# A two-layer trunk on one core: two PSUM banks each for transposes and attention outputs, earlier raw weight loads, and sums of squares issued in smaller pieces

## The chip, the cores and the metric

The kernel runs on one core of one Trainium2 chip. The number compared is the device time of one execution in microseconds. The kernel before took 2080.81 us, the median of three runs from 2080.38 to 2085.92 us. Beside these there is one profiled execution, from which every row below comes.

A core has a matrix engine (TensorE: PE in the rows, PEld for its weight loads), VectorE (DVE), ScalarE (ACT), GpSimd (POOL) and SyncE (SP), which here only issues transfers. TensorE writes only to PSUM, which holds eight banks of 128 x 512 floats. VectorE and ScalarE empty the banks. Each engine runs its own instructions in the order in which the program has them, and waits on semaphores for the others.

## The reference

The input is one sequence of 1024 tokens with 1024 features, and 256 memory tokens. Two layers follow each other. In each, the stream is RMS-normed and put through one input projection. One half of the heads is a token mixer (a gated linear recurrence in layer 0, forgetting attention in layer 1), the other half is a cross-attention into the memory. Both outputs are concatenated, put through an output projection and added to the stream. Then a squared-ReLU MLP of width 4096 is added. In short:

```
for layer in range(2):
    h = rms_norm(x, norm_mix[layer])
    y_mix, xq = rglru_group(h, ...) if layer == 0 else fox_group(h, ...)
    y_mem = memory_group(xq, mem, ...)
    x = x + concat([y_mix, y_mem]) @ w_out[layer]
    x = x + square(relu(rms_norm(x, norm_mlp[layer]) @ w1)) @ w2

# fox_group, one block of queries
s = q @ k.T * scale + c[q] - c[k];  s = where(causal, s, -1e30)
o = softmax(s) @ v
```

All of it is in float32. The forgetting attention has 8 heads of 64 features, and the cross-attention 4 heads of 128.

## The kernel before

**Numbers.** Every operand of a product is kept as a rounded high part and a low part, and a product is three matmuls (high x high, high x low, low x high). A tile to be split is copied by ScalarE into the high part, and VectorE subtracts it to get the low part (`split_sb`, `split`, and for weights `_wpart`, lines 320 and 321).

**Stages.** The sequence is worked in two halves of 512 tokens (h = 0 and 1). In order of time: layer 0's projections, recurrence and cross-attention for both halves; its output projection (`outproj`, then `outproj2` for the second half); the MLP of layer 0 (`mlp`, about 345 to 927 us); layer 1's projections (`fox_proj`, `xq_proj`), its cross-attention (`xattn`) and forgetting attention (`fox`); its output projection; the MLP of layer 1 (from about 1465 us). The MLP treats its matrices as 2 x 2 blocks and computes them with seven block products instead of eight (`product`, line 1066), in eight groups g = 0 to 7, each with `mlp_z` (first matrix) and `mlp_out` (second).

**The forgetting attention.** For each head `fox_scores` computes four rows of scores (L1477, mask L1479) into an `s` bank. VectorE adds the decay and takes the minimum in one custom instruction (L1482), ScalarE takes the exponential with its sum (L252), VectorE the reciprocal (L1492), and GpSimd scales the row (L1494). `fox_pv` then turns these rows: for each block of 128 keys it transposes up to four 128 x 128 pieces into a `pt` bank (L1519), ScalarE copies the bank to the high part (L1522), VectorE subtracts for the low part (L1523), and two matmuls (L1509 with the high part, L1510 with the low) add the block into the head's `o` bank. At the end of a head ScalarE and VectorE empty the `o` bank (L1535, L1536). `fox_pair` (L1436, L1447) turns queries and keys of two heads through `pt` banks. In the first half a head has 4 key blocks, in the second 8.

**What sets the order.** The program is written as generators that are woven into each other: a stage of projections or output products runs as the main stream, and attention is advanced beside it at rates from the table `TUNE`. From the written program a scheduler then makes each engine's final order, moving an instruction where its operands and a free buffer are expected. A PSUM tile takes its bank from its tag's own small pool, `PB = {"pj": 2, "s": 2, "pt": 3, "o": 1}`: a third `pt` tile can be open while two are being emptied, but the next head's first L1509 must wait until the one `o` bank is empty. Matmuls of projections and of the MLP that are placed between attention's instructions are called filler below: they need nothing from the attention.

**Weights.** Raw chunks of 128 x 1024 floats go by SyncE's queue into three or four raw buffers (`_wraw`, L316), are split into one of three high and low buffers, and are then used. `_wraw(self.wload + 2)` issues loads for chunks less than two ahead of the last one split, and never into a buffer whose chunk isn't split yet. Layer 1's weights that both halves use are written to memory once split and read back.

**Sums of squares.** For the norm ahead of an MLP, `sq_pe` squares the eight tiles of the second half and `sq_mm` adds each by four matmuls with one output column (L467) into an `o` tile. Before, `sq_mm` is called inside the MLP's first group (in `hook0`) and around the waiting products in `mlp`.

**The last group of layer 0's MLP.** `held` keeps the first half of the stream in on-chip tiles `xres`: `plus` on VectorE (L1082) adds the first use of each bank into the tile, and later the second use. Elsewhere the first use is a ScalarE copy (`copies`, L1077), and the second is added to the copy.

Of the kernel before, what the change touches and what calls it, by code (L numbers as in the profile page):

```python
# [126 lines left out]
def chain(*gs):  # L127
# [33 lines left out]
    "cp_f00": 0,  # L161
    "cp_f01": 1,
    "cp_f10": 1,
    "cp_f11": 1,
    "cp_kv0": 1,
# [10 lines left out]
class Builder:  # L176
    NU = 86
    NRING = 3
    PB = {"pj": 2, "s": 2, "pt": 3, "o": 1}

    def __init__(self, ctx, tc, ins, out):
# [45 lines left out]
        warm = self.psum("pt")  # L227
        for _ in range(8):
            nc.tensor.matmul(warm[:, :P], lhsT=self.ones, rhs=self.ones, start=True, stop=True)
# [93 lines left out]
    def _wsplit(self, upto):  # L323
        nc = self.nc
        while self.wload < min(len(self.plan), upto):
# [19 lines left out]
            self.wload += 1  # L345
            self._wraw(self.wload + 2)

# [103 lines left out]
    def sq_pe(self, m, h, xt, behind=None):  # L451
        sq = self.F.get()
        i = self.nc.scalar.activation(sq[:, :H], xt, AF.Square)
        if behind is not None:
            self.after(i, behind)
        if m == 0:
            self.stp[h] = [None, []]
        self.stp[h][1].append((m, sq))

    def sq_mm(self, h, keep):  # L460
# [501 lines left out]
    def outproj2(self, h, k0, k1, src, gain, side):  # L962
        nc = self.nc
        tags = ["pj", "pj", "s", "s", "pt", "pt", "pt"]
        n = len(tags)
# [236 lines left out]
    def mlp_out(self, l, g, mid, side=None):  # L1202
# [28 lines left out]
        def held(a):  # L1231
            def first(q, ps):
                self.plus(self.xres[2 * q + a], ps)

            def then(q, ps):
                x = self.xres[2 * q + a]
                self.plus(x, ps)
                nc.sync.dma_start(self.xs[2 * q + a, :, :H], x[:, n])

# [31 lines left out]
        A = [self.psum(k) for k in ("s", "s", "pj", "pj")]  # L1271
        more = ("pt", "pt", "pt", "o")
        c11, c21, c22 = keep(0, 0), keep(1, 0), keep(1, 1)
# [11 lines left out]
    def mlp(self, l, wait, nxt=None):  # L1285
# [3 lines left out]
        def hook0(key):  # L1289
            if key in ahead:  # L1290
                self.xsplit(ahead[key])
            if key in ("b11", "b21"):
                self.sq_mm(1, 6 if key == "b11" else 3)
            if key in ("t2", "t3"):
                advance(nf)

        def hook7(key):
# [4 lines left out]
            if key == "t1" and l:  # L1302
                self.acc = [self.load_x(2 * q, 0, self.xs) for q in range(4)]

        for p in wait:
            for k in ("t3", "t1"):
                self.xsplit(k)
            self.sq_mm(1, 5)
            drain(p)
            self.sq_mm(1, 2)  # L1310
        for g in range(8):
            if g == 0 and g in self.parked:
                for k in ("t3", "t1"):
                    self.xsplit(k)
            drain(self.mlp_z(l, g, hook0 if g == 0 else hook7 if g == 7 else lambda key: None))
            if g == 7:
# [549 lines left out]
```

## Time and profile before

| | |
|---|---|
| median of three runs | 2080.81 us |
| the profiled execution | 2081.96 us |
| its span, first to last instruction | 2080.3 us |
| TensorE busy | 2046.6 us, 98% of the span |
| VectorE, ScalarE, GpSimd busy | 75%, 55%, 22% |
| mean granted TensorE clock | 0.996 |

A row of grouped instructions reads: line, engine, operation, output<-inputs (buffer numbers left out), shape, count | busy time, mean ns of one | idle time of the engine just before them and what ended it. A row of waits reads: who <- whom, us in total, times, longest. A row of the timeline reads: start, duration, engine, line, what, count, and in brackets the idle time just before and what ended it. A row of windows reads: stretch and length, then busy time with count for PE, PEld, DVE, ACT and POOL, the granted clock, the DMA engines' busy share and GB/s. Matmuls are pipelined, so their durations overlap: the distance from start to start counts, not the duration of one.

### The profile page before, as it was taken

How to read it: one execution, taken by the hardware profiler on the slowest of the kernel's cores; microseconds unless marked ns; L12 is line 12 of the kernel's file. 1: busy time of each engine (PE TensorE's matmuls, PEld its weight loads, DVE VectorE, ACT ScalarE, POOL GpSimd, SP SyncE). 2: the span in 40 equal slices, each digit the busy share in tenths (PEclk: the TensorE clock that was granted, in tenths of full speed). 3: DMA queues.
4: the chain of work that ended last, by engine and by line, in shares of the span. 5: the costliest groups of instructions: out<-in, count | busy, mean ns of one | idle time of the engine just before them, and what ended most of it. 6: DMA issues, size and time to landing. Idle time of an engine off the chain costs nothing. (4 is left out here: it accounts for less than half of the span.)

```text
span 2080.3 us, 29644 instructions
## 1 busy us (share of the span) xinstructions
PE 2046.6 (98%) x10378; PEld 1706.1 (82%) x10378; DVE 1569.0 (75%) x2924; ACT 1148.5 (55%) x2164; POOL 456.6 (22%) x582
## 2 busy tenths in 40 slices
PE   9999999999999999999999999999999999999999
PEld 7998778888788878879998998777778888888887
DVE  7897698776766776778685779686886767758757
ACT  7856655554553554547555646575655545545543
POOL 1022220202202201204442423232021222022021
PEclk9999999999999999999999999999999999999999
DMA  8433261635635635737767437644356575265274
GB/s 294 150 95 119 100 208 61 132 81 112 132 81 111 132 81 112 160 103 224 274 240 272 138 118 283 228 134 150 101 119 143 129 167 115 71 139 113 70 182 121
DMA packets 122645, 301.55 MB, mean 145 GB/s; under 512 B 13760, under 2 KB 15872, under 8 KB 122496
## 3 DMA queue, kind: packets, MB, share of 16 engines
q1 hardware_dynamic: 80736, 211.50, 30.1%
q0 software_dynamic: 41760, 88.16, 22.3%
q8 instruction: 81, 1.33, 0.3%
q14 instruction: 68, 0.56, 0.1%
HBM read 190.46 MB, written 109.15 MB: 144 GB/s over the span
## 5 line engine op out<-in xcount | busy, mean ns | idle before, releaser
L1066 PE MATMUL pspt<-r,wh 128*128 128x512 f32 x1536 | 493.4, 397 | 6.4 <-DVE f L1082 2.9
L321 DVE TENSOR_TENSOR wl<-wr,wh 128x1024 fp32r<-128x1024 f32 (+2 forms) x354 | 338.3, 964 | 182.7 <-ACT wh L320 181.5
L320 ACT ACTIVATE wh<-wr 128x1024 fp32r<-128x1024 f32 (+3 forms) x403 | 303.5, 776 | 301.6 <-PE pss L1066 77.0
L1222 POOL DMA_DIRECT2D xspill<-f x232 | 203.1, 1071 | 871.6 <-DVE f L1082 802.5
L1066 PEld LDWEIGHTS pspt<-r,wh 128*128 128x128 f32 x1536 | 288.2, 188 | 78.6 <-ACT r L500 4.3
L1066 PE MATMUL pss<-r,wh 128*128 128x512 f32 x1024 | 328.4, 397 | 0.5 <-DVE r L503 0.4
L1066 PE MATMUL pspt<-r,wl 128*128 128x512 f32 x768 | 304.0, 396 | 0.7 <-DVE wl L321 0.7
L1066 PE MATMUL pspj<-r,wh 128*128 128x512 f32 x832 | 273.6, 402 | 0.9 <-DVE r L495 0.7
L389 PE MATMUL pspj<-wh,r 128*128 128x256 f32 (+1 forms) x1280 | 244.3, 285 | 2.1 <-DVE fl L1390 0.8
L503 DVE TENSOR_TENSOR r<-f,r 128x512 fp32r<-128x512 f32 x282 | 188.6, 685 | 71.8 <-DMA xspill<-f 52.0
L1066 PEld LDWEIGHTS pss<-r,wh 128*128 128x128 f32 x1024 | 192.5, 188 | 48.3 <-DVE r L503 1.3
L500 ACT ACTIVATE r<-f 128x512 fp32r<-128x512 f32 x282 | 169.2, 625 | 79.0 <-DMA xspill<-f 20.4
L389 PEld LDWEIGHTS pspj<-wh,r 128*128 128x128 f32 x1280 | 201.8, 189 | 4.7 <-PE pspj L389 1.0
L1066 PE MATMUL pss<-r,wl 128*128 128x512 f32 x512 | 202.7, 396 | 0.0
L1066 PEld LDWEIGHTS pspj<-r,wh 128*128 128x128 f32 x832 | 157.0, 190 | 40.3 <-DVE r L495 1.6
L389 PE MATMUL pspj<-wl,r 128*128 128x256 f32 (+1 forms) x640 | 182.2, 285 | 0.6 <-DVE wl L321 0.3
L1066 PEld LDWEIGHTS pspt<-r,wl 128*128 128x128 f32 x768 | 144.5, 188 | 36.1 <-DVE wl L321 1.1
L1066 PE MATMUL pspj<-r,wl 128*128 128x512 f32 x416 | 165.4, 398 | 0.0
L389 PE MATMUL pspj<-r,wh 128*128 128x512 f32 x480 | 158.6, 406 | 1.8 <-ACT wh L320 0.9
L1087 ACT ACTIVATE f<-f 128x512 f32<-128x512 f32 x128 | 78.7, 626 | 109.2 <-DVE f L1086 107.0
L389 PEld LDWEIGHTS pspj<-wl,r 128*128 128x128 f32 x640 | 120.8, 189 | 1.6 <-DVE wl L321 0.5
L1066 PEld LDWEIGHTS pss<-r,wl 128*128 128x128 f32 x512 | 96.3, 188 | 23.4
(301 smaller groups left out, 3555.9 us busy)
## 6 DMA issues: line engine op xcount, KB each, us to landing
wr<-in_w_dram SPq DMA_DIRECT2D x136, 512.0 KB, 4.0
xspill<-f POOLq DMA_DIRECT2D x232, 256.0 KB, 7.4
f<-xspill SPq DMA_DIRECT2D x88, 256.0 KB, 4.7
xspill<-f SPq DMA_DIRECT2D x56, 256.0 KB, 3.2
wsp<-wh SPq DMA_DIRECT2D x22, 512.0 KB, 5.7
wsp<-wl SPq DMA_DIRECT2D x22, 512.0 KB, 6.1
wh<-wsp POOLq DMA_DIRECT2D x21, 512.0 KB, 5.7
wl<-wsp POOLq DMA_DIRECT2D x21, 512.0 KB, 5.6
```

The lines of the kernel that those rows point to most:

```text
L320: self.wact = self.nc.scalar.activation(hi, raw, AF.Copy)
L321: eng.tensor_tensor(lo, raw, hi.bitcast(F32), ALU.subtract)
L389: self.lastmm = self.nc.tensor.matmul(out, lhsT=a, rhs=b, start=(j == 0), stop=(j == n - 1))
L500: i = self.nc.scalar.activation(hi[:, :n], src, AF.Copy)
L503: self.nc.vector.tensor_tensor(lo[:, :n], src, hi[:, :n].bitcast(F32), ALU.subtract)
L1066: self.lastmm = self.nc.tensor.matmul(ps, lhsT=a, rhs=b, start=(start and c == 0 and j == 0), stop=(c == n - 1 and j == 2), skip_group_che ...
L1087: self.lastsq = self.nc.scalar.activation(f[:, n], f[:, n], AF.Square)
L1222: nc.gpsimd.dma_start(self.xs[2 * q + a, :, b * H:(b + 1) * H], f[:, n], accum_op=ALU.add)
```

## The change

It has six parts. (1) `PB` becomes two `pt` banks and two `o` banks; the places that named three `pt` tiles and one `o` (`outproj2`, `mlp_out`) now name two and two, or use an `o` for the last one. (2) Raw loads may be issued for chunks less than four ahead. (3) `sq_pe` calls `sq_mm` itself and keeps at most four squares back; `feed` issues one square at each step of the waiting products and of the MLP's groups, and the calls in `hook0` and `mlp` go. (4) In `held` the first use of a bank is a ScalarE copy; after the second use VectorE adds the bank, and then the copy, into `xres`. (5) Three of layer 1's four projections copy their raw PSUM tiles by ScalarE (L601) and no longer by VectorE (L599). (6) Ten warm-up matmuls stand at the start and not eight.

```
-    "cp_f01": 1,
-    "cp_f10": 1,
-    "cp_f11": 1,
+    "cp_f01": 0,
+    "cp_f10": 0,
+    "cp_f11": 0,
...
-    PB = {"pj": 2, "s": 2, "pt": 3, "o": 1}
+    PB = {"pj": 2, "s": 2, "pt": 2, "o": 2}
...
-        for _ in range(8):
+        for _ in range(10):
             nc.tensor.matmul(warm[:, :P], lhsT=self.ones, rhs=self.ones, start=True, stop=True)
...
             self.wload += 1
-            self._wraw(self.wload + 2)
+            self._wraw(self.wload + 4)
...
         self.stp[h][1].append((m, sq))
+        self.sq_mm(h, 4)
...
-        tags = ["pj", "pj", "s", "s", "pt", "pt", "pt"]
+        tags = ["pj", "pj", "s", "s", "pt", "pt", "o"]
...
         def held(a):
-            def first(q, ps):
-                self.plus(self.xres[2 * q + a], ps)
+            dst = []
+            first = self.copies(dst)
 
             def then(q, ps):
                 x = self.xres[2 * q + a]
                 self.plus(x, ps)
+                self.plus(x, dst[q][:, n])
+                self.F.put(dst[q])
                 nc.sync.dma_start(self.xs[2 * q + a, :, :H], x[:, n])
...
-        more = ("pt", "pt", "pt", "o")
+        more = ("pt", "pt", "o", "o")
...
-            if key in ("b11", "b21"):
-                self.sq_mm(1, 6 if key == "b11" else 3)
...
+        def feed(p):
+            for _ in p:
+                if 1 in self.stp:
+                    self.sq_mm(1, max(0, len(self.stp[1][1]) - 1))
...
-            self.sq_mm(1, 5)
-            drain(p)
-            self.sq_mm(1, 2)
+            feed(p)
...
-            drain(self.mlp_z(l, g, hook0 if g == 0 else hook7 if g == 7 else lambda key: None))
+            feed(self.mlp_z(l, g, hook0 if g == 0 else hook7 if g == 7 else lambda key: None))
```

Counted over the built programs, instructions change by kind only in (4), (5) and (6): VectorE loses 24 copies of 128 x 256, and ScalarE gets 24 of them and 8 copies of 128 x 512; eight of VectorE's additions read an on-chip tile where they read a bank. The matmuls are the same but for the two warm-ups. What moves is the order. From line 459 on, lines of the changed kernel are numbered one higher than before (L1509 is L1513 from line 1233 on). In the rows below, `pt`, `pj`, `s` and `o` after `ps` are the tags, and the number is that of the tile.

TensorE where the seventh head of the first half gives way to the eighth (time 1201 to 1204 us in the profile before). Before, the last filler and the eighth head's first products, with the `o` tile 11717:

```order
L389 MATMUL pspj_12041<-wl_77,r_1033_10211 128x264
L389 MATMUL pspj_12041<-wh_74,r_1034_10212 128x264
L1509 MATMUL pso_11717<-r_1190_11723,r_1035_10278 128x512
L1510 MATMUL pso_11717<-r_1191_11724,r_1035_10278 128x512
L1509 MATMUL pso_11717<-r_1193_11747,r_1036_10306 128x384
L1519 MATMUL pspt_11795<-ident,f_1185_11654 128x128
```

With the change, the same place, with the `o` tile 11735:

```order
L389 MATMUL pspj_12633<-wh_74,r_1011_9981 128x256
L1513 MATMUL pso_11735<-r_1198_11741,r_1043_10297 128x512
L389 MATMUL pspj_12633<-wl_77,r_1011_9981 128x256
L389 MATMUL pspj_12633<-wh_74,r_1012_9982 128x256
L389 MATMUL pspj_12633<-wh_74,r_1016_10019 128x256
L389 MATMUL pspj_12633<-wl_77,r_1016_10019 128x256
L389 MATMUL pspj_12633<-wh_74,r_1017_10020 128x256
L389 MATMUL pspj_12633<-wh_74,r_1021_10057 128x256
L389 MATMUL pspj_12633<-wl_77,r_1021_10057 128x256
L389 MATMUL pspj_12633<-wh_74,r_1022_10058 128x256
L1514 MATMUL pso_11735<-r_1199_11742,r_1043_10297 128x512
```

The product with the high part and that with the low part now have filler between them, and the `o` tile is in the bank that the head before does not use.

VectorE in the last group of layer 0's MLP (time 914 to 928 us before). Before, from the first additions of the banks `s` and `pj` on; `L1082` in each row is `plus`:

```order
L1082 TENSOR_TENSOR f_830_7865<-f_830_7865,pss_8006 128x512
L1187 TENSOR_TENSOR f_816_7732<-f_842_7970,f_816_7732 128x512
L1082 TENSOR_TENSOR f_832_7869<-f_832_7869,pspj_8008 128x512
L503 TENSOR_TENSOR r_841_7953<-f_823_7822,r_840_7952 128x512
L1082 TENSOR_TENSOR f_831_7867<-f_831_7867,pss_8007 128x512
L1187 TENSOR_TENSOR f_817_7746<-f_846_7992,f_817_7746 128x512
L1082 TENSOR_TENSOR f_833_7871<-f_833_7871,pspj_8009 128x512
```

With the change, the stretch that ends with the first addition from a `pt` bank, which before came nine rows behind the piece above:

```order
L504 TENSOR_TENSOR r_863_8115<-f_816_7734,r_862_8114 128x512
L504 TENSOR_TENSOR r_865_8119<-f_817_7748,r_864_8118 128x512
L504 TENSOR_TENSOR r_845_7979<-f_843_7976,r_844_7978 128x512
L1083 TENSOR_TENSOR f_830_7867<-f_830_7867,pspt_8057 128x512
L504 TENSOR_TENSOR r_857_8062<-f_842_7972,r_856_8061 128x512
L1083 TENSOR_TENSOR f_831_7869<-f_831_7869,pspt_8058 128x512
L1083 TENSOR_TENSOR f_832_7871<-f_832_7871,pso_8059 128x512
L1199 TENSOR_TENSOR f_823_7825<-f_823_7825,f_847_7998 128x512
L1083 TENSOR_TENSOR f_833_7873<-f_833_7873,pso_8060 128x512
```

From the low part of a weight that both programs split just ahead (`wl_77`) to this first addition, 16 instructions stand before and 14 with the change: the four additions from `s` and `pj` are gone, and one split (L504) and one subtraction (L1199) have come ahead of it.

TensorE in the second half of the forgetting attention. Before, ahead of the sixth head (about 1404 us), where transposes of one head go to three tiles in turn, with filler around them:

```order
L1066 MATMUL pspj_14842<-r_1504_14384,wh_75 128x512
L1519 MATMUL pspt_14246<-ident,f_1467_14137 128x128
L1519 MATMUL pspt_14255<-ident,f_1467_14137 128x128
L1519 MATMUL pspt_14295<-ident,f_1467_14137 128x128
L1066 MATMUL pspj_14842<-r_1505_14385,wh_75 128x512
L1066 MATMUL pspj_14842<-r_1504_14384,wl_78 128x512
```

With the change, where one of the heads without filler gives way to the next:

```order
L1523 MATMUL pspt_13688<-ident,f_1387_13514 128x128
L1523 MATMUL pspt_13688<-ident,f_1395_13579 128x128
L1513 MATMUL pso_13399<-r_1399_13608,r_1242_12290 128x128
L1514 MATMUL pso_13399<-r_1400_13609,r_1242_12290 128x128
L1523 MATMUL pspt_13697<-ident,f_1367_13381 128x128
L1523 MATMUL pspt_13697<-ident,f_1374_13434 128x128
L1523 MATMUL pspt_13697<-ident,f_1387_13514 128x128
L1523 MATMUL pspt_13697<-ident,f_1395_13579 128x128
L1481 MATMUL pss_13719<-r_1110_10905,r_1380_13479 128x512
L1481 MATMUL pss_13719<-r_1110_10905,r_1381_13480 128x512
L1513 MATMUL pso_13687<-r_1410_13693,r_970_9578 128x512
```

The transposes fill one tile, then the other, and no third; the next head's output has its own bank. Of the eight heads of the second half, counted from a head's first product to the next head's, three (the second, the third and the sixth) now have none of the filler matmuls (L389, L1066 before) between them; before, the head with the fewest has 12 (the sixth). The attention of the end of the first half stands up to 180 rows later against the projections, and has caught up again by the fourth head of the second half.

## The prediction

> **What bounds the kernel now.** I read the busy shares first, then a stretch of MLP in the chain of waits, then the waits of TensorE summed by releaser (who <- whom), and last the windows and timelines around those waits.
>
> ```profile
> PE 2046.6 (98%) x10378; PEld 1706.1 (82%) x10378; DVE 1569.0 (75%) x2924; ACT 1148.5 (55%) x2164; POOL 456.6 (22%) x582
> 1560.46 5.60 PE pspt L1066 x24
> PE pss L1477 <- DVE mn L1482: 4.7, 9, 1.3
> PE pspt L1066 <- DVE f L1082: 2.9, 2, 2.3
> PE pso L1509 <- DVE f L1536: 1.7, 1, 1.7
> ```
>
> TensorE bounds it. A matmul with 512 columns goes by every 5.60 / 24 = 0.233 us, and over the whole span TensorE idles 2080.3 − 2046.6 = 33.7 us. Since the change removes no matmul, it can win only there or where the clock is lower. The named idle places are few: in sum 4.7 us behind the attention's decay addition (L1482), 2.9 behind `plus` at the end of layer 0's MLP, 1.7 behind the emptying of the one `o` bank. Behind two of them the clock falls:
>
> ```profile
> 924.90:928.40 3.50, 1.90 (x5) 0.95 (x6) 3.50 (x7) 0.89 (x2) 0.00 (x0) 1.00 0.44 165
> 928.40:931.90 3.50, 3.50 (x10) 2.72 (x9) 3.50 (x7) 0.23 (x1) 0.00 (x0) 0.51 0.57 162
> 1201.50:1204.90 3.40, 1.65 (x10) 1.08 (x8) 3.40 (x6) 0.92 (x3) 0.39 (x1) 1.00 0.02 5
> 1204.90:1208.40 3.50, 3.50 (x19) 3.50 (x18) 2.22 (x8) 1.47 (x3) 0.00 (x0) 0.51 0.00 0
> 1471.20:1474.60 3.40, 3.40 (x9) 2.65 (x9) 3.40 (x7) 1.26 (x2) 0.00 (x0) 0.50 0.20 77
> 1484.80:1491.70 6.90, 6.12 (x14) 4.08 (x15) 6.25 (x11) 3.82 (x7) 0.00 (x0) 0.51 0.29 106
> ```
>
> After a stretch with 1.6 to 1.9 us idle, the next 3.4 us have a granted clock of 0.51. At that clock 3.4 us hold the work of 1.7, so such a period costs at most 1.7 us; I take 1.5, for the part in which TensorE would wait anyway. There are five such periods (the last row holds two).
>
> **The change part by part.** The sum is made against the profiled execution, 2081.96 us, which is 1.15 above the median of the three runs.
>
> *`held` (4).*
>
> ```profile
> 925.65 0.47 PE L1066 MATMUL pspt<-r,wh 128*128 128x512 f32 x1 [2.26 <-DVE f L1082]
> 924.84 0.67 DVE L1082 TENSOR_TENSOR f<-f,pspt 128x512 f32<-128x512 f32 x1
> 926.04 1.27 DVE L1082 TENSOR_TENSOR f<-f,pspt 128x512 f32<-128x512 f32 x2
> ```
>
> TensorE waits 2.26 us until VectorE reaches the first addition from a `pt` bank. VectorE is the late one: it has no gap here, and starts one of these instructions every 0.60 us (924.84 and 926.04, with one between). By the order shown above, 16 of its instructions stand ahead of that addition and 14 with the change: −1.2 us. The bounds are 0 (the two that are newly ahead wait for ScalarE) and −2.9, both waits. ScalarE has to fit in four copies; it is busy 55% of the span and 0.89 of the 3.50 us from 924.9, so it should have room, and if it hasn't, the wait goes over to it. With the gap under about half of its size, the window at 924.9 has 2.4 us busy and I expect no half clock: −1.5, between 0 and −1.5. The eight extra additions on VectorE come after the banks are free; no matmul waits for `xres` then.
>
> *Second `o` bank (1).*
>
> ```profile
> 1203.78 0.47 PE L1509 MATMUL pso<-r,r 128*128 128x512 f32 x1 [1.71 <-DVE f L1536]
> 1200.30 2.74 DVE L1372 TENSOR_TENSOR f<-f,fr 128x512 f32<-128x512 f32 x3
> 1202.97 0.67 DVE L1536 TENSOR_TENSOR f<-f,pso 64x512 f32<-64x512 f32 x1
> ```
>
> Here the emptying of the bank (L1536) stood behind three additions that take 2.74 us, and the next head's first product waited 1.71 us. With two banks it need not wait, and by the order filler stands between the products too: −1.7 (0 if the wait goes over to the `pt` banks), and the half-clock period from 1204.9 goes with it: −1.5 (0 to −1.5).
>
> *Raw loads (2).*
>
> ```profile
> 276.16 3.45 SPq L542 DMA_DIRECT2D f<-xspill  x3
> 279.71 0.37 SPq L316 DMA_DIRECT2D wr<-in_wout_dram  x1
> 283.68 0.63 ACT L320 ACTIVATE wh<-wr 128x512 fp32r<-128x512 f32 x1 [2.21 <-DMA wr<-in_wout_dram]
> 284.36 0.74 PE L978 MATMUL pspt<-r,wh 128*128 128x512 f32 x2 [0.57 <-ACT wh L320]
> ```
>
> A weight chunk of layer 0's output projection was issued behind three loads of the stream, its split waited 2.21 us for it, and TensorE 0.57. With the change this load stands ahead of those: −0.6, 0 to −0.6. The price: the load of a buffer waits on SP's queue until that buffer is split, and the stream's loads queue behind it. In the MLP a stream load has whole block products to land, so I take 0; if each of the two layers has one late as here, it is +1.1.
>
> *Two `pt` banks in the attention (1).* The first half has filler nearly everywhere. The second half doesn't:
>
> ```profile
> 1257.00:1453.00 196.00, 187.27 (x1002) 152.63 (x1002) 151.58 (x376) 122.62 (x273) 59.92 (x89) 1.00 0.59 201
> 1405.00:1423.00 18.00, 15.37 (x87) 12.29 (x87) 14.60 (x47) 11.94 (x32) 6.98 (x12) 1.00 0.30 102
> L389 PE MATMUL pspj<-r,wh 128*128 128x512 f32 x139 | 46.0, 404 | 0.2 <-ACT r L500 0.2
> L1066 PE MATMUL pspj<-r,wh 128*128 128x512 f32 x112 | 38.6, 409 | 0.7 <-DVE r L495 0.7
> L389 PE MATMUL pspj<-r,wl 128*128 128x512 f32 x69 | 27.6, 400 | 0.0
> L1066 PE MATMUL pspj<-r,wl 128*128 128x512 f32 x56 | 22.1, 394 | 0.0
> L389 PE MATMUL pspj<-wh,r 128*128 128x256 f32 x53 | 10.2, 284 | 0.0
> L1523 DVE TENSOR_TENSOR r<-pspt,r 128x512 fp32r<-128x512 f32 (+1 forms) x64 | 36.0, 583 | 9.4 <-ACT r L1522 9.2
> L1482 DVE CUSTOM_DVE_ANT_0 f<-pss,f 128x512 f32<-128x512 f32 x32 | 21.9, 684 | 0.6 <-DMA f<-cscr 0.5
> L1482 DVE CUSTOM_DVE_ANT_0 f<-pss,f,mn 128x128 f32<-128x128 f32 (+3 forms) x32 | 17.4, 544 | 4.8 <-DMA f<-cscr 3.2 <-PE pss L1479 1.2
> L1490 DVE TENSOR_TENSOR fsm<-fsm 128x1 f32<-128x1 f32 x32 | 6.3, 197 | 2.8 <-ACT f L252 2.6
> L1452 DVE SCALAR_TENSOR_TENSOR r<-pspt,gk,r 64x512 fp32r<-64x512 f32 x8 | 6.0, 750 | 0.3
> L1536 DVE TENSOR_TENSOR f<-f,pso 64x512 f32<-64x512 f32 x8 | 5.5, 683 | 5.4 <-ACT f L1535 5.3
> L1442 DVE SCALAR_TENSOR_TENSOR r<-pspt,par,r 64x512 fp32r<-64x512 f32 x7 | 5.2, 750 | 1.4 <-ACT r L1441 1.2
> L1482 DVE DVE_READ_ACCUMULATOR2_ANT mn<- 128x1 f32 x64 | 5.2, 82 | 0.0
> L1492 DVE RECIPROCAL frc<-fsm 128x1 f32<-128x1 f32 x32 | 5.1, 160 | 1.7
> ```
>
> These 196 us hold the eight heads; TensorE idles 8.7 us in them. Filler is 376 matmuls at 0.233 and, with half as many for the low part as the 53 shown, 79 of 256 columns at half of that: 87.6 + 9.2 = 96.8 us, which leaves (187.3 − 96.8) / 8 = 11.3 us of TensorE per head. VectorE's own rows for the attention (the last nine) sum to 108.6, or 13.6 per head. So a head without filler is set by VectorE, and TensorE idles 2.3 us in it even where VectorE never stops. VectorE does stop for ScalarE's copy ahead of L1523: 9.4 us, 1.2 a head; with a `pt` bank less to run ahead in, I take 0.8 of this into the head: 3.1 idle. Three heads have lost all their filler: 9.3 us. The 8.7 of now came mostly from the same limit in heads with little filler; with the filler now in the other five I let it go altogether: +0.6. From below, all idle but the three heads' 2.3 goes and the clock is better: 6.9 − 8.7 = −1.8. From above, a head lasts as long as the worst stretch of now, 18 us from 1405: see the third rival.
>
> *Parts at nothing.*
>
> ```profile
> 1150.00:1200.00 50.00, 50.00 (x403) 48.93 (x403) 42.27 (x143) 33.02 (x88) 21.58 (x35) 1.00 0.49 160
> 1.12 3.78 PE L229 MATMUL pspt<-ones 128*128 128x128 f32 x16 [1.12 <-DVE halo L815]
> 5.79 1.22 PE L389 MATMUL pspj<-r,wh 128*128 128x512 f32 x2 [0.89 <-ACT wh L320]
> ```
>
> (5) moves 24 copies of some 0.4 us off VectorE: in the first half's attention VectorE is busy 42 of 50 us and ScalarE 33, and TensorE waits for neither (50.00 busy). If ScalarE's ten more microseconds fell ahead of an exponential, they would show as VectorE's wait on it. (6) adds two matmuls (16 records for eight, 0.47 each): 0.94 in a gap of 0.89 in which TensorE waits for the first weight. (3) leaves its blocks at the start of layer 1's MLP almost as they are in the order, 12, 4, 8 and 8 products of L467 in one piece; if they were spread, the three half-clock periods from 1471 would go, −4.5. In the MLP four banks are emptied in about four times 0.6 us, while the next product runs 5.6, so two `pt` and two `o` do what three and one did.
>
> Sum: −1.2 − 1.5 − 1.7 − 1.5 − 0.6 + 0.6 = −5.9. 2081.96 − 5.9 − 1.15 = **2074.9 us** for the median.
>
> On the clock, the Trainium skill (page "TensorE: Matmul & The Clock Gate", Part 1: The HAM clock gate) says that the half rate comes after at least one idle window of about 3.4 us, and warns of gaps over that. This trace differs: stretches of 3.4 us that are half busy are followed by 0.51. By the page's rule gaps of this size would not move the clock, the two terms of 1.5 would be 0, and the time that of the second rival.
>
> **The rivals.** *The attention gains too.* Two `o` banks let the next head's scores and products start under the emptying of the last, and the idle 8.7 halves (−4.4 and not +0.6), and two of the three late half-clock periods go (−3.0): −13.9, **2066.9**. For it: L1536 waits 5.4 us on ScalarE's copy in these heads. Against: VectorE's 13.6 per head stays, and three heads have no filler.
>
> *The gaps go, the clock stays.* The half-clock periods move to other gaps: the sum is −1.2 − 1.7 − 0.6 + 0.6 = −2.9, **2077.9**. For it: there are periods after 1471 and 1484 that I cannot tie to one wait. Against: two of the five follow a gap that I can name.
>
> *Two transposing banks starve the heads without filler.* L1519 of the next block waits until L1523 has emptied the bank two back; with the third bank gone this is met at each block of the three heads (2, 3 and 6 of the second half). If each lasts 18 us, as 1405 to 1423 does, TensorE idles 18 − 11.3 = 6.7 in each, and being under two thirds busy it falls to half clock once per head (1.5): 3 × 8.2 − 8.7 = +15.9 in place of +0.6, sum +9.4, **2090.2**. It makes the kernel slower from heads of 16.9 us on. For it: TensorE idled 2.6 of 18 us there with three banks and some filler. Against: the chain of one block (0.6 for the copy, 0.6 for the subtraction) is shorter than a block's share of VectorE, 13.6 / 8 = 1.7, so two banks should feed it.
>
> **How the numbers follow.** Forecast 0.48, attention gains 0.17, clock stays 0.13, starved heads 0.22. A measurement of this kernel can tell about 0.3%, 6.2 us, from no change: faster is below 2074.6, slower above 2087.0. The forecast, at 2074.9, lies on that line: 0.24 faster, 0.24 the same. With the first rival 0.41 faster, with the second 0.37 the same, with the third 0.22 slower. The likeliest case's own range is 2070 to 2080, from its bounds; the range for 8 in 10 reaches to the first rival and almost to the third: 2065 to 2088.
>
> **What would show it.** Right: no wait at the first `pt` product near 924 above 1.1 us and clock 1.00 after it; no wait L1509 <- L1536; heads 2, 3 and 6 of the second half at about 14.4 us with waits of L1477 on L1482, not of L1519 on L1523; TensorE idle about 9 us in the second half. Wrong: waits L1519 <- L1523 (1523 and 1527 then) over 5 us, half-clock periods inside the second half's heads, waits of stream or `cscr` loads on SP behind raw loads, or ScalarE's copies at 916 to 924 late.

## The result, and the profile after

| | before | changed |
|---|---|---|
| median | 2083.36 us (4 runs, 2080.38 to 2086.63) | 2110.18 us (4 runs, 2107.93 to 2112.93) |
| ratio | | 1.013, 95% interval 1.0117 to 1.0142 |
| profiled execution | 2081.96 us | 2107.93 us |
| mean granted clock | 0.996 | 0.991 |

The change makes the kernel 27 us slower. The forecast was 2074.9 us, with a range up to 2088; it named the direction wrongly. The page of the changed kernel begins with its busy row, and the rows below it are from TensorE's waits over the whole span:

```profile
PE 2057.3 (98%) x10382; PEld 1710.6 (81%) x10382; DVE 1563.3 (74%) x2900; ACT 1164.2 (55%) x2196; POOL 449.9 (21%) x582
PE pss L1481 <- DVE mn L1486: 9.1, 9, 2.0
PE pspj L389 <- DVE wl L321: 4.4, 5, 2.0
PE pspt L389 <- DVE wl L321: 2.5, 1, 2.5
PE pspt L1523 <- DVE r L1446: 2.5, 2, 1.9
PE pso L1513 <- ACT r L1526: 1.8, 1, 1.8
```

(L1481, L1486, L1513 and L1523 are the L1477, L1482, L1509 and L1519 of before.) The wait for the emptied `o` bank (L1509 on L1536, 1.7 us) is gone, and of the 2.9 us behind `plus` 0.5 are left. TensorE's idle time has nevertheless grown from 33.7 to 2106.2 − 2057.3 = 48.9 us, and its busy time by 11 us, although it has only two more matmuls. That second part is the clock: at half clock a matmul is busy for longer.

Where the time went is seen by setting the same matmul of both traces against each other, the n-th of its line in order of time (the matmuls of L1066 are those of the MLPs):

| TensorE reaches | before, us | changed, us | late by |
|---|---|---|---|
| in layer 0's first output projection (L389, 1051st) | 238.1 | 239.3 | 1.3 |
| first product of `outproj2`, layer 0 (L978) | 259.9 | 275.2 | 15.3 |
| layer 0's MLP, 201st matmul of L1066 | 369.2 | 380.5 | 11.3 |
| end of that MLP's middle (2401st) | 883.1 | 893.9 | 10.8 |
| after its last group (2601st) | 935.4 | 941.3 | 5.9 |
| layer 1's first score (L1477) | 1116.4 | 1124.3 | 7.9 |
| first product of the second half's heads (L1509, 33rd) | 1286.0 | 1325.5 | 39.5 |
| layer 1's MLP (L1066, 3201st) | 1567.8 | 1593.9 | 26.1 |
| last matmul | 2075.3 | 2101.4 | 26.2 |

So there are two losses, of about 10 us at layer 0's output projection and of about 18 us in layer 1's attention up to the start of its MLP, and one gain of 5 us at the end of layer 0's MLP; 1.3 us come before these and 2 in layer 1's projections. (The 39.5 us at the first head of the second half is not all lost: filler that before stood behind that point has been done ahead of it.) The windows of the changed kernel show how: first the output projection of layer 0, then heads 1 to 6 of the second half, each from its first product to the next head's, and last all eight heads together (columns as in the windows of the prediction):

```profile
250.00:300.00 50.00, 43.78 (x181) 33.56 (x180) 40.53 (x67) 23.20 (x37) 5.52 (x6) 0.97 0.52 169
1325.50:1348.50 23.00, 19.59 (x97) 15.30 (x96) 15.16 (x31) 16.10 (x29) 4.52 (x8) 0.93 0.48 151
1348.50:1364.60 16.10, 13.83 (x73) 10.84 (x71) 12.08 (x42) 10.29 (x30) 5.85 (x10) 0.89 0.11 33
1364.60:1384.40 19.80, 14.39 (x64) 9.97 (x63) 13.16 (x35) 13.75 (x30) 3.76 (x6) 0.81 0.08 28
1384.40:1410.60 26.20, 26.20 (x134) 21.89 (x133) 20.24 (x62) 17.10 (x41) 10.06 (x16) 0.95 0.44 109
1410.60:1433.40 22.80, 21.40 (x115) 16.95 (x113) 19.21 (x51) 16.32 (x36) 5.10 (x9) 1.00 0.49 154
1433.40:1445.40 12.00, 10.02 (x59) 7.57 (x58) 9.08 (x29) 8.60 (x24) 4.30 (x7) 1.00 0.14 44
1325.00:1480.00 155.00, 140.31 (x707) 110.75 (x705) 106.76 (x282) 98.31 (x219) 40.76 (x67) 0.94 0.35 106
```

The heads without filler (2, 3 and 6: second, third and sixth row of the heads) last 16.1, 19.8 and 12.0 us, and TensorE idles 2.3, 5.4 and 2.0 us in them. VectorE isn't full in them either: 13.16 of 19.8 us in head 3. Over the heads the idle time is 155.0 − 140.3 = 14.7 us. Before, the same stretch, from 1286 to 1451 us, had 7.7:

```profile
1286.00:1451.00 165.00, 157.30 (x823) 126.98 (x822) 122.89 (x305) 103.20 (x228) 48.50 (x76) 1.00 0.54 183
```

The clock column is the other half: 1.00 before, 0.94 now. 0.06 of 155 us is 9 us of work not done, at most, since TensorE also idles in these periods. In heads 2, 3 and 6 VectorE waits for the decay rows, 3.3, 2.3 and 1.7 us of the 4.0, 6.6 and 2.9 that it idles there; in head 3 more of its waiting is for ScalarE's copies (3.2 us, L1527 on L1526). This is its timeline in heads 2 and 3 of the changed kernel, with the row of the queue that brings the rows:

```profile
1356.23 23.88 SPq L1466 DMA_DIRECT2D f<-cscr  x3
1359.17 0.69 DVE L1486 CUSTOM_DVE_ANT_0 f<-pss,f 128x512 f32<-128x512 f32 x1 [1.73 <-DMA f<-cscr]
1360.60 0.35 DVE L1486 CUSTOM_DVE_ANT_0 f<-pss,f,mn 128x128 f32<-128x128 f32 x1 [0.73 <-DMA f<-cscr]
1382.74 0.69 DVE L1486 CUSTOM_DVE_ANT_0 f<-pss,f 128x512 f32<-128x512 f32 x1 [1.79 <-DMA f<-cscr]
```

At the start of a head's scores VectorE stands still for the load, the scores' bank isn't emptied, and TensorE waits behind it (1.95 and 1.70 us at 1359.9 and 1383.5). The waits of VectorE and of SP over the second half sum to the first four rows; the last row is that of before:

```profile
DVE r L1527 <- ACT r L1526: 13.2, 14, 2.3
DVE f L1486 <- DMA f<-cscr: 10.0, 9, 1.8
SPq L1466 <- PE pspt L1523: 32.6, 4, 15.0
SPq L1466 <- PE pso L1514: 25.8, 2, 22.4
DVE f L1482 <- DMA f<-cscr: 3.7, 3, 3.2
```

The load itself waits on SP, by the rows mostly for transposes and products of earlier heads (L1523, L1514), before a buffer is free for it.

In layer 0 the trace suggests a chain of engines that each work in order. In time order, in the changed kernel:

```profile
251.47 2.56 ACT L252 ACTIVATE f<-f,sp 128x512 f32<-128x512 f32 x4 [2.17 <-PE pso L760]
252.28 1.23 POOL L893 TENSOR_SCALAR f<-f 128x512 f32<-128x512 f32 x2 [3.97 <-ACT f L252]
253.53 2.50 DVE L894 SCALAR_TENSOR_TENSOR f<-f,f 128x512 f32<-128x512 f32 x4 [4.71 <-POOL f L893]
262.03 1.21 DVE L321 TENSOR_TENSOR wl<-wr,wh 128x1024 fp32r<-128x1024 f32 x1
263.30 0.50 PE L389 MATMUL pspt<-r,wl 128*128 128x512 f32 x1 [2.48 <-DVE wl L321]
```

The cross-attention's product comes late, so ScalarE's exponentials of the recurrence wait for it in their order, GpSimd for ScalarE, VectorE for GpSimd, and the split of the next weight (L321) stands behind that work on VectorE. TensorE waits 2.48 us for the split, and a half-clock period follows (264.0 to 267.4 us).

### The profile page after: what moved, and what is told of

Read it like the earlier page. It is cut to its first block, busy times and chain, and to the rows that moved or that the text cites. A ratio compares the mean times of both kernels' runs of the same rounds, so it can differ in the third digit from the quotient of the medians.

```text
span 2106.2 us, 29646 instructions
## 1 busy us (share of the span) xinstructions
PE 2057.3 (98%) x10382; PEld 1710.6 (81%) x10382; DVE 1563.3 (74%) x2900; ACT 1164.2 (55%) x2196; POOL 449.9 (21%) x582
## 4 chain that ended last, share of the span: by engine, by line
PE 43%; DVE 4%; ACT 3%; issue 2%; DMA 2%; POOL 0%; ACTq 0%; DVEq 0%; POOLq 0%; SPq 0%
PE pspj L389 10%; PE pspt L1067 10%; PE pss L1067 8%; PE pspj L1067 7%; PE pso L1067 3%; PE pss L1481 1%; PE pspt L1523 1%; DMA f<-cscr 1%; ACT f L252 1%; PE pso L1514 1%; DVE wl L321 1%; PE pso L1513 1%; PE pso L760 0%; DVE r L504 0%; PE pss L382 0%
## 5 line engine op out<-in xcount | busy, mean ns | idle before, releaser
L321 DVE TENSOR_TENSOR wl<-wr,wh 128x1024 fp32r<-128x1024 f32 (+2 forms) x354 | 338.9, 967 | 190.4 <-ACT wh L320 187.1
L1067 PE MATMUL pspt<-r,wh 128*128 128x512 f32 x1344 | 433.3, 398 | 3.3 <-DVE r L504 1.9
L1067 PEld LDWEIGHTS pspt<-r,wh 128*128 128x128 f32 x1344 | 252.8, 189 | 66.2 <-DVE r L504 3.5
L1067 PE MATMUL pspj<-r,wh 128*128 128x512 f32 x832 | 269.1, 397 | 0.1
L1067 PE MATMUL pspt<-r,wl 128*128 128x512 f32 x672 | 266.6, 397 | 1.1 <-DVE wl L321 1.1
L389 PE MATMUL pspj<-wh,r 128*128 128x256 f32 (+1 forms) x1280 | 243.9, 284 | 4.5 <-ACT f L602 2.1
L504 DVE TENSOR_TENSOR r<-f,r 128x512 fp32r<-128x512 f32 x282 | 189.0, 687 | 75.6 <-DMA xspill<-f 44.1
L501 ACT ACTIVATE r<-f 128x512 fp32r<-128x512 f32 x282 | 168.9, 625 | 71.5 <-DMA xspill<-f 26.1
L389 PEld LDWEIGHTS pspj<-wh,r 128*128 128x128 f32 x1280 | 201.5, 189 | 6.7 <-ACT f L602 2.7
L389 PE MATMUL pspj<-wl,r 128*128 128x256 f32 (+1 forms) x640 | 181.5, 284 | 2.4 <-DVE wl L321 1.6
L389 PE MATMUL pspj<-r,wh 128*128 128x512 f32 x480 | 156.8, 403 | 1.8 <-ACT r L493 1.2
L1067 PEld LDWEIGHTS pspt<-r,wl 128*128 128x128 f32 x672 | 126.8, 189 | 32.2 <-DVE wl L321 1.5
L1067 PE MATMUL pso<-r,wh 128*128 128x512 f32 x384 | 128.4, 396 | 0.5 <-DVE f L1083 0.5
L389 PEld LDWEIGHTS pspj<-wl,r 128*128 128x128 f32 x640 | 120.5, 188 | 3.7 <-DVE wl L321 2.5
```

Source lines behind the costliest of these rows:

```text
L321: eng.tensor_tensor(lo, raw, hi.bitcast(F32), ALU.subtract)
L389: self.lastmm = self.nc.tensor.matmul(out, lhsT=a, rhs=b, start=(j == 0), stop=(j == n - 1))
L501: i = self.nc.scalar.activation(hi[:, :n], src, AF.Copy)
L504: self.nc.vector.tensor_tensor(lo[:, :n], src, hi[:, :n].bitcast(F32), ALU.subtract)
L1067: self.lastmm = self.nc.tensor.matmul(ps, lhsT=a, rhs=b, start=(start and c == 0 and j == 0), stop=(c == n - 1 and j == 2), skip_group_che ...
```

## The experiments

Each time is compared with runs of the kernel before on the same chip, whose median lay between 2083.4 and 2085.0 us.

**The banks alone (1).** The edit is the three changed lines of the banks in the kernel before.

> The kernel before with part (1) alone: two pt and two o banks. By its order the second half's heads 2, 3 and 6 already have 0 filler matmuls. Theory A (the banks cost about 16 us in layer 1's attention, the earlier raw loads about 11 us in layer 0's output projection, and held gives 5 back): about 2083 + 16 = 2099 us, TensorE waiting on VectorE's L1482 in those heads, four or five half-clock periods in the second half, and layer 0's output projection (first product of it at 260 us before) at most 2 us late. Rival B (the banks cost both, since layer 0's output projection uses pt banks too): about 2110 us, first product of layer 0's output projection at about 275. Rival C (the attention is late for the copies moved to ScalarE, not for the banks): about 2083.

Measured: 2121.08 us, 1.0181 (1.0166 to 1.0196). Layer 0's `outproj2` starts at 278.0 us, 18.1 late, layer 0's MLP runs 14 late, and layer 1's MLP 36. Rival B holds, with 11 us more than it expected: the banks cost both losses, and more than the whole change does.

**The raw loads alone (2).** `_wraw(self.wload + 4)` in the kernel before.

> The kernel before with part (2) alone: raw loads for chunks less than four ahead. Theory A: about 2083 + 11 = 2094 us, with a stretch of over 10 us on SP in which a raw load waits on a split and loads of the stream stand behind it, and ScalarE's L492 waiting over 5 us for such a load; the attention as before. Rival B: 2083, layer 0's output projection as before or 0.6 us better.

Measured: 2084.10 us, 0.9999 (0.9988 to 1.0010). No stage is more than 2.2 us from the kernel before. Theory A falls; it had put layer 0's loss on the loads because in the changed kernel SP issues nothing for 14 us from 246 on.

**All but the banks.** The changed kernel with `{"pj": 2, "s": 2, "pt": 3, "o": 1}` and the tags of before.

> The changed kernel with three pt banks and one o bank again. Theory A: 2110 - 16 = about 2094 us, the loss left in layer 0's output projection (its first product near 275 us). Rival B: 2110 - 27 - 5 = about 2078, since only the gain at the end of layer 0's MLP is left. Rival C: about 2110. By the order its third head of the second half has 3 filler matmuls and the sixth 6, so some of the attention's loss (up to 5 us) can stay under A.

Measured: 2081.63 us, 0.9994 (0.9985 to 1.0004). Layer 0's loss is gone (MLP at −0.1 us at the 2401st matmul), the gain at the MLP's end is there (−5.1 at the 2601st), but in the attention it is given back: +1.8 us at layer 1's MLP. So it is 3.6 us slower than Rival B expected.

**All but the loads.** `self.wload + 2` in the changed kernel.

> The changed kernel with raw loads less than two ahead again. Theory A: 2110 - 11 = about 2099 us, layer 0's output projection as before and the attention's loss in full. Rival B: about 2110.

Measured: 2112.82 us, 1.0145 (1.0124 to 1.0165). Rival B again.

**Which bank, and where.** The next three kernels have two `pt` banks and one `o`; the eighth bank gets a tag `x` of its own, which stands for the third `pt` tile in the MLP and in `outproj2`. In the second and third, every third tile of the transposes goes to `x` in one layer:

```
PB = {"pj": 2, "s": 2, "pt": 2, "o": 1, "x": 1}
...
def psum(self, tag, fixed=False):
    if tag == "pt" and self.three and not fixed:
        self.turn += 1
        tag = "x" if self.turn % 3 == 0 else "pt"
```

> The kernel before with two pt banks and still one o bank; the eighth bank x is used only where an MLP or outproj2 names its third pt tile. Theory D (the third transposing bank is what is missed, the second o bank is not what harms): as with both edits, about 2083 + 36 = 2119 us, layer 0's output projection starting 15 us late, no filler in heads 2 and 3 of the second half. Rival E (the second o bank changes the order for the worse): about 2083.

> The same bank x, but in layer 1 up to the end of its attention every third pt tile goes to it, so that three banks take transposes there, and two in layer 0. Theory D with two separate places: layer 0's loss stays (first product of its output projection near 275, +14), the attention's goes (the heads' filler is near that of before): about 2097 us. If the attention is late only since layer 0 was late or for the second o bank, it is about 2119.

> The reverse: three banks take transposes in layer 0 and two in layer 1. Theory D with two separate places: first product of layer 0's output projection at about 260 as before, the attention's loss in full: 2083 + 22 = about 2105 us. If layer 1's loss only follows from layer 0's, about 2083.

Measured: 2113.53 us (1.0146; 1.0126 to 1.0167), 2093.40 us (1.0050; 1.0035 to 1.0066) and 2108.83 us (1.0124; 1.0107 to 1.0141). Theory D holds. The third transposing bank is what is missed, and in each layer for itself: with three banks in layer 1 only, layer 0's MLP runs 6.8 us late; with three in layer 0 only, it runs 1.9 late and layer 1's MLP 25.7. In the former the attention isn't quite as before: layer 1 goes from 7.7 late at its first score to 13.4 at its MLP, so the fixed turn of the three banks leaves about 6 of 24 us. The second `o` bank makes up for nothing: with it and two `pt` banks the time was 2121, without it 2113.5.

**Held alone (4).**

> The kernel before with part (4) alone. If the gain of 5 us at the end of layer 0's MLP is that of the ScalarE copies and the half-clock period behind them, and the later loss of the kernel with all but the banks came from the copies of part (5), it is about 2083 - 5 = 2078 us, with full clock after 924 us. If the gain is taken back in the attention whatever the copies, 2083.

Measured: 2082.64 us, 0.9991 (0.9980 to 1.0002). In its place the gain is whole. In the profiled run TensorE is 1.7 us late at the 2401st matmul of L1066 and 3.3 early at the 2601st, and the stretch that had idled is full, at full clock:

```profile
921.50:931.90 10.40, 9.97 (x43) 7.76 (x42) 10.40 (x18) 5.36 (x10) 0.00 (x0) 1.00 0.17 53
```

But that run has half-clock periods at 9, 278, 326, 1357 and 1497 us that the profiled run of before has not, and over ten runs the median is only 1 us lower: nothing that this measurement can tell.

**Who holds the bank in layer 0.** The kernel with two `pt` and one `o`, where layer 0's first output projection takes its third bank from `x`:

> The kernel with two pt banks and one o bank, but layer 0's first output projection takes its third bank from x and no longer from pt, so that the cross-attention beside it has both pt banks for its transposes. Theory F (the output projection's tile holds one of the two pt banks for 24 matmuls, and the transposes are left with one): layer 0's part of the loss goes (first product of outproj2 at about 261 us and not 270, first MLP product no more than 2 us late), 2113.5 - 5 = about 2108 us. If transposes lack the third bank themselves, it stays at about 2113.

Measured: 2112.27 us, 1.0131 (1.0115 to 1.0147). `outproj2` starts 9.6 us earlier than before, but layer 0's MLP still runs 6.2 late (7.0 without the edit). Theory F falls: the loss only moves into `outproj2`.

**VectorE's work in the heads.** The subtraction for the attention's low part is left out, and the second product uses the high part again; once with two `pt` banks and one `o`, once on the kernel before.

```
-            ph, pl = self.R.get(), self.R.get()
+            ph = self.R.get()
+            pl = ph
...
-            nc.vector.tensor_tensor(pl[:, c], pt[:, c], ph[:, c].bitcast(F32), ALU.subtract)
```

> Two pt banks and one o bank; in the forgetting attention VectorE's subtraction for the low part (L1523 of the kernel before) is left out, and the second product uses the high part again, so TensorE has the same matmuls and VectorE 0.58 us x 64 less in the second half, 4.5 us per head. The heads 2 and 3 have no filler here either. Theory G (a head without filler lasts as long as VectorE's work): it is now 13.6 - 4.5 = 9.1 us of VectorE against at most 11.3 of TensorE, so the idle time in these heads goes, and the attention's loss of about 22 us against the same edit on the kernel before falls under 6; in all within 12 us of the next run, with layer 0's 7 still in it. Rival H (TensorE waits for the transposing banks themselves): still about 30 us above the next run.

> The kernel before with the same edit: VectorE's subtraction for the low part of the attention's weights left out, the second product with the high part. As the base for the run ahead of it. By theory G some of the 8.7 us idle in the second half goes: 2083 - 5 = about 2078; by rival H 2083.

Measured: 2097.12 us (1.0060; 1.0043 to 1.0078) and 2083.24 us (0.9993; 0.9984 to 1.0002). The 29.8 us between two and three `pt` banks have shrunk to 14, of which 6.6 are layer 0's. Of 24 us in layer 1 about 8 are left, so two thirds of the loss go with VectorE's subtraction, though more is left than theory G expected, and with three banks the edit wins nothing where G expected 5 us. The edit also empties each `pt` bank one instruction sooner, so by itself it doesn't part VectorE's work from the time for which a bank is held; for the work speaks that with two `pt` banks and one `o` TensorE waits 8.5 us for L1482 in the second half, and 3.4 with its transposes for a bank. In heads 2 and 3 of the first of these kernels VectorE still waits:

```profile
DVE f L1482 <- DMA f<-cscr: 5.3, 2, 4.9
DVE fsm L1490 <- ACT f L252: 2.2, 4, 1.1
```

**The decay rows one head earlier.** In the changed kernel, and in the kernel with two `pt` banks and without the subtraction:

```
-        ck = self.fox_ck(h, hd)
+        ck = self.early.pop((h, hd), None) or self.fox_ck(h, hd)
+        if h and hd < 7:
+            self.early[(h, hd + 1)] = self.fox_ck(h, hd + 1)
```

> The changed kernel, but in the second half each head's decay rows are loaded one head earlier (two more buffers in use). The heads without filler stay without it. Theory I (VectorE's 10.0 us of waits for these rows between 1325 and 1480 are part of what sets these heads): the waits go, and with them 5 to 10 us: about 2103 us. Theory G alone (VectorE's work sets the heads whatever the rows): the waits are taken over by other work, 2110.

> Two pt banks and one o bank, VectorE's subtraction in the attention left out as in the two kernels without the low part, and the decay rows one head earlier. If G and I together are the whole of the attention's loss, the 8 us left in layer 1 fall under 3: 2097 - 6 = about 2091 us, of which 7 over the base are layer 0's. If not, 2097.

Measured: 2101.21 us (1.0082; 1.0068 to 1.0095), 9 us less than the changed kernel, and 2091.58 us (1.0036; 1.0026 to 1.0046). Theory I holds: the late rows are part of what sets the changed kernel's heads. Whether they are part of what the banks cost is another question, which the last run below bears on. In the first, VectorE's 10.0 us of waits for these rows are gone from this stretch, although heads 2, 3 and 6 have no filler as before, and TensorE idles 8.1 us there and not 14.7:

```profile
1325.00:1475.00 150.00, 141.92 (x733) 112.76 (x732) 113.41 (x288) 99.99 (x222) 41.98 (x67) 0.98 0.37 113
```

The second is to be compared with the kernel with three banks and without the subtraction: it is 4.1 us behind that one at the 2401st matmul of L1066, 4.5 at the 2601st, and 6.4 at layer 1's MLP. What is left to layer 1 is about 2 us in the profiled runs, and about 4 by the medians. That VectorE's work and the late load together are layer 1's loss isn't shown by this: its rows are loaded late, and the early rows were not run with three banks and without the subtraction.

**The copies alone (5), and the parts that are left.**

> The kernel before with part (5) alone: the raw copies on ScalarE. By its order the third and the sixth head of the second half have 3 and 6 filler matmuls, before 42 and 12. If this is what took held's gain back: 2083 + 5 = about 2088 us; if the copies cost nothing as forecast, 2083.

> The kernel before with parts (2), (3), (4) and (6), without the banks and without the copies of part (5). By the order its heads have the filler of the kernel before. If the copies of part (5) are what took the 5 us of held back in the attention, 2083 - 5 = about 2078 us, faster than both kernels; if not, about 2082 as with held alone.

> The kernel with parts (2), (3), (4) and (6) alone, with the decay rows one head earlier. Three transposing banks leave filler in most heads, and VectorE's waits for these rows are 3.7 us in the second half of the kernel before: 0 to -3, 2077 to 2080 us.

Measured: the copies alone 2093.92 us, 1.0044 (1.0030 to 1.0058), a loss twice as large as expected. Parts (2), (3), (4) and (6) together 2079.61 us, 0.9970 (0.9960 to 0.9981). The same with the decay rows one head earlier 2072.26 us, 0.9937 (0.9924 to 0.9949), which beats both kernels, by more than expected.

This last pair bears on what the early rows show. They win 7 us here, with three `pt` banks, against 9 in the changed kernel. From the first score to the start of layer 1's MLP they take 452.3 us to 444.9 here, and 469.6 to 461.6 there: the distance between the two kernels, which differ in the banks and the copies, is 17.3 us with late rows and 16.7 with early ones. So the late load costs time in both, and explains little of what the change loses. In the kernel with parts (2), (3), (4) and (6) VectorE waited for it too, by this row of its second half:

```profile
DVE f L1486 <- DMA f<-cscr: 6.5, 3, 5.5
```

The copies cost nothing where they are made; they shift the order, so that head 3 of the second half has 3 filler matmuls and not 42. In the kernel with the copies alone that head looks like those of the changed kernel, with 2 us idle and a clock of 0.82:

```profile
1352.80:1371.40 18.60, 16.61 (x83) 12.90 (x82) 16.22 (x41) 15.73 (x36) 4.10 (x7) 0.82 0.24 70
```

In the fastest kernel TensorE idles 3.9 us in the second half's attention, at full clock, and the busy row of its page shows 99%:

```profile
1282.00:1445.00 163.00, 159.15 (x836) 130.09 (x835) 122.65 (x304) 103.76 (x231) 48.58 (x74) 1.00 0.56 177
PE 2041.6 (99%) x10382; PEld 1705.5 (82%) x10382; DVE 1568.7 (76%) x2924; ACT 1152.9 (56%) x2172; POOL 452.6 (22%) x582
```

## Why the prediction was wrong

**`held`: VectorE's part was right, the size too small.** The terms were −1.2 and −1.5. Four profiled kernels show −4.9 to −5.0 between the 2401st and the 2601st matmul of L1066 (changed, held alone, all but the banks, all but banks and copies). The clock's part came as forecast: the half-clock period behind 924 is gone. VectorE's part did too: its first addition from a `pt` bank stood 1.85 us behind the start of TensorE's last matmul ahead of the wait (924.84 and 922.99), and now stands 0.68 behind it (934.52 and 933.84), 1.2 us sooner. What the sum didn't have is TensorE's order: twelve products into `s` and `pj` banks now stand ahead of the first `pt` product and cover the rest, and only 0.42 us of waiting is left there:

```profile
933.61 0.63 PE L1067 MATMUL pspj<-r,wh 128*128 128x512 f32 x2
934.66 0.50 PE L1067 MATMUL pss<-r,wh 128*128 128x512 f32 x1 [0.42 <-DVE r L504]
937.56 0.63 PE L1067 MATMUL pspt<-r,wh 128*128 128x512 f32 x2
```

**The second `o` bank: right at its place, and of no use in sum.** The wait on L1536 and the half clock behind it are gone. But two `pt` banks with one `o` were faster than with two, 1.0146 against 1.0181 of the kernel before, or 7 us, with intervals that just touch.

**Raw loads:** alone they moved the median by +0.7 us; an effect of the forecast size, −0.6, is below what these runs can tell.

**Two `pt` banks in the attention: the step that failed.** The sum had +0.6, the trace shows about +18 between the first score and layer 1's MLP. The mechanism was named, heads that lost their filler are set by VectorE, and for TensorE's idle time in the three heads it even gave the right sum: 9.3 us forecast, 9.7 measured. That is in part luck, since the heads last 16.1, 19.8 and 12.0 us and not 14.4 each. What failed is the rest of the term:

- The 8.7 us of idle time in the heads of before were let go altogether, since the filler is now in the other five heads. These five idle 5.0 us. In sum the heads idle 7.0 us more than before (14.7 and 7.7).
- The clock was counted only as something to win. Five half-clock periods came into these heads, before there was none: at most 9 us of lost work.
- VectorE's 13.6 us per head were taken as gapless but for 0.8 us of ScalarE's waits. The row of L1482 quoted for this sum had 3.2 us idle behind `f<-cscr`, and this wait was not followed: it is 10.0 us now. The runs with early rows show its price, 9 us, but nearly the same price with three banks, so it is no large part of the difference.

The idle time and the clock together are most of the 18 us; the rest is not traced. Of the cause, the runs show that the third transposing bank is missed (24 us in layer 1 where it alone is taken) and that 16 of these 24 us go with VectorE's subtraction; the other 8 stay open. The third rival, with 18 us for such a head and one half-clock period in each, gave +15.9, near what was measured, but by other parts: it had 20.1 us idle in the three heads and none in the others, and it put the wait on the wrong bank. TensorE waits mostly with its scores (L1481 on L1486, 9.1 us over the whole span), and with the transposes for a bank to be emptied only 2.5 us (L1523 on L1446). What changed with the bank is the order. Heads 1 to 3 of the second half have 31, 0 and 0 filler matmuls, and had 72, 62 and 42; that filler is put in the transposes' place because they find no bank is argued, not shown.

**Layer 0 was not costed.** The sum looked at `pt` tiles in layer 1 only. Layer 0's cross-attention and output projections use the same banks, and the loss there, 10 to 14 us with two `o` banks and 7 with one, is missing from the prediction as a term and as a rival. The comparison of the orders was made for layer 1 alone. That the bank causes it is shown by the two runs with three banks in one layer; which wait starts the chain at 251 us is argued from the trace only, since the run with a bank of its own for the output projection did not settle it.

**The copies were put at nothing.** Their cover was named rightly, ScalarE has room and TensorE waits for none of them. But moved instructions shift the order of everything else, and alone they cost 9.6 us. This step had the same blind spot as the banks: where does the filler lie afterwards?

**Spread sums of squares and warm-ups** were not run alone; with the loads and `held` they are in the kernel that gained 5.4 us. As forecast, the three half-clock periods at the start of layer 1's MLP are still there in the changed kernel (two from 1506.5 us, one from 1520.1).

## What to carry to other kernels

Where a scheduler sets the order, a smaller pool can act on the order long before engines wait much for a bank: after such an edit count the filler between the dependent pieces, in every stage that uses the pool, and cost the pieces that have lost it with all their waits, those for small loads too. A stage without filler pays twice, by its idle time and by the half clock behind it. And of a change with six parts, the harmful ones can hide good ones: two of the parts cost 38 and 10 us alone, and the other four gained 5.

## What the runs showed of the hardware

Half-clock periods aren't a fixed property of a program. Over 68 runs of the unchanged kernel the mean granted clock lay between 0.990 and 0.996, and the time went with it: 2082.2 us on average at 0.996 (5 runs), 2083.7 at 0.994 (13 runs), 2085.5 at 0.992 (15 runs). That is part of the spread of some 10 us between runs of one kernel, and not all of it: at 0.993 alone the times go from 2083.5 to 2090.5. In the changed kernel the granted clock was low around waits of 1 to 2 us each, as in these two windows:

```profile
1373.50:1380.50 7.00, 5.10 (x18) 3.56 (x18) 3.62 (x8) 3.53 (x7) 1.36 (x2) 0.52 0.02 9
1383.50:1387.00 3.50, 3.50 (x12) 3.03 (x13) 3.05 (x9) 1.20 (x4) 0.00 (x0) 0.51 0.00 0
```

No TensorE wait in the eight heads of the second half is longer than 2.0 us, and still there are five half-clock periods of 3.4 us in them: here, idle time spread over a stretch is enough. How much is seen by cutting the 18 kept traces into stretches of 3.41 us, the length of most half-clock periods, on the grid on which these periods begin, past the first 15 us. Of the stretches at full clock in which TensorE was busy for less than half, 57 of 60 were followed by half clock; of those busy for 70 to 90%, 3 of 312. Of 10,221 busier ones 18 were, and in all of these TensorE had 20 or more products with one output column (L467, 0.11 us each): such work kept it busy and didn't keep the clock. In the kernel before they stand just ahead of the period from 1471:

```profile
1468.39 2.73 PE L467 MATMUL pso<-cD,f 128*128 128x1 f32 x24
```

The table of states in the Trainium skill ("TensorE: Matmul & The Clock Gate", Part 1: The HAM clock gate) puts the half rate behind at least one idle window of about 3.4 us. The measurement decides: no such window stands before the periods in the heads. By that row of the Trainium skill the two terms of the clock in the prediction would have been 0, and the loss in the heads only their idle time.
